# A diffusion transformer on one core: the first four chunks of the first stage one at a time

## The chip, the cores and the metric

The kernel runs on one core of a Trainium2 chip. The metric is the device time of one execution in microseconds. Engines are called by the names of the profile: PE is TensorE (matrix products), DVE VectorE, ACT ScalarE, POOL GpSimd, SP SyncE, whose queue issues most loads.

## What is computed

Two layers of a transformer on 256 latent tokens (x) and 256 context tokens (ctx) of 1024 features. Each layer first modulates its input with a scale and a shift per feature that come from a product of a conditioning vector with the adaLN weights (ada_w), then mixes tokens (retention in layer 0, neighbourhood attention in layer 1) and applies an MLP. The change is in the very first steps of layer 0:

```python
mod = (silu_c @ ada_w[i] + ada_b[i])[:, None, :]
mod_c = silu_cc @ ada_w[i] + ada_b[i]
sh1, sc1, g1, sh2, sc2, g2 = jnp.split(mod, 6, axis=-1)
...
h = x * (1.0 + sc1) + sh1
hc = ctx * (1.0 + sc1c) + sh1c
...
p = h @ w
q = heads(p[..., :qk_w], RET_QK_DIM)
...
v = heads(p[..., 2 * qk_w:2 * qk_w + v_w], RET_V_DIM)
```

All is in 32-bit floats. Each product with weights is done as three products of a rounded high part and a remainder (hi and lo of the weights, hTh and hTl of the tokens).

## The kernel before

The first stage computes, for head 0 of the retention, the query projection (256 columns, accumulated in the two banks pq) and the value projection (512 columns, accumulated for four groups of 128 tokens in the four banks pv). The 1024 features that both sum over are cut into eight chunks of 128. A chunk needs: its part of the shift and scale weights of adaLN (2 x 1024 x 128 floats, 1.05 MB), 128 columns of x and ctx (0.26 MB), and 128 rows of the projection weights (0.39 MB).

The work is done in quarters of two chunks (line 938). A quarter's adaLN weights come in four loads of 512 KB (tile rawq), its tokens in two loads (R), its projection weights in two (raw). For a quarter the engines do this:

- PE multiplies the adaLN weights by the conditioning columns cT in 32 short products that write into four strips of a bank (quarter_sums, line 802; tile pada). The profile counts each as two instructions, hence x64.
- DVE copies the sums out (quarter_row, tile row), PE adds the strips and turns the result into columns with two small products (quarter_columns, line 828, pada<-cst,row), and DVE adds the bias (tile mod).
- PE transposes the tokens of a chunk (chunk, tile pt).
- ACT and DVE modulate them (modulate_chunk, line 862): ACT writes both halves of hTh, DVE and ACT a half each of aff, DVE takes the difference to hTl. Each of these waits for the one before it.
- ACT rounds the projection weights (tile hi), DVE takes the remainder (lo).
- PE does the query products of a chunk (quarter_q, six of 512 columns) and its value products (quarter_v, three for each of the four token groups, a value block below).

The order on PE, ACT, DVE and SP in this stage is the order of the code. Value blocks of the chunk before are placed between the steps of the next quarter's modulation, so that PE has work while the chain from sums to modulated tokens runs through the other engines. The first quarter has nothing ahead of it: PE turns over products of a constant tile (turn_over, pq<-still) while it waits for loads. Loads are issued by SP in the order of need, a quarter or more ahead; a load waits where the tile that it fills is still in use. Raw projection weights have four buffers, adaLN quarters two slots (AQ), each of two tiles.

From line 996 on the same order of instructions holds on each engine with and without the change.

Of the kernel before, what the change touches and what calls it, by code (L numbers as in the profile page):

```python
# [10 lines left out]
F32 = mybir.dt.float32  # L11
# [6 lines left out]
P = 128  # L18
D = 1024
KC = D // P  # L20
# [73 lines left out]
def kernel(  # L94
# [50 lines left out]
    def bank(s="ps"):  # L145
        return psp.tile([P, 512], F32, tag="ps", name=nm(s))
# [104 lines left out]
            pending.append((lo[:], raw[:], hi[:]))  # L251
            units.append((hi, lo))

    def load():

        src, k, ncol = specs[loaded[0]]
        loaded[0] += 1
        raw = rawp.tile([P, k, ncol], F32, tag="raw", name=nm("raw"))
        sp.dma_start(out=raw[:], in_=src.rearrange("(k p) n -> p k n", p=P))

        def begin():
            hi = hip.tile([P, k, ncol], F32R, tag="hi", name=nm("hi"))
# [9 lines left out]
            return high, low  # L272

        return begin

    def lows(n=100, eng=None):
# [461 lines left out]
    pq = [bank("pq") for _ in range(2)]  # L738
    AQ = ((S_GS, S_SH), (S_SL, S_VH))

    def quarter_x(i, q):
        for a, src in enumerate((x, ctx_in)):
            cols = slice(256 * i, 256 * i + 256)
            q.dma_start(out=RR[a][:, :, cols], in_=src[0][:, cols].rearrange("(t p) c -> p t c", p=P))

    def quarter_loads(i):
        raws = ada_quarter_load(i, AQ[i % 2])
        quarter_x(i, sp)
        return raws

# [71 lines left out]
    def quarter_rows(i, raws):  # L822
        pr = bank("pada")
        for s in range(2):
            quarter_sums(pr, raws, s, range(KC))
        return pr, quarter_row(pr)
# [43 lines left out]
    def modulate_kinds(k, pts, between=lambda: None):  # L870

        tmp = scr("aff")
        for e, a in ((act, 0), (dve, 1)):
            modulated(e, hTh[:, k, KINDS[a]], pts[a][:, :NLAT], k, a)
        between()
        for e, a in ((act, 1), (dve, 0)):
            modulated(e, tmp[:, KINDS[a]], pts[a][:, :NLAT], k, a)
        dve.tensor_sub(out=hTl[:, k, :], in0=tmp[:], in1=hTh[:, k, :].bitcast(F32))

    def quarter_q(k, kk, wq, terms=range(3)):  # L880
        wh, wl = wq
        hh, hl = hs(k, 0, NT)
        for i in terms:
            w, h = ((wh, hh), (wl, hh), (wh, hl))[i]
            for dc in range(2):
                pe.matmul(
                    pq[dc][:], lhsT=w[:, kk, tsl(dc)], rhs=h, start=(k == 0 and i == 0), stop=(k == KC - 1 and i == 2)
                )
# [8 lines left out]
            for f in parts:  # L897
                f(k)

    raws = ada_quarter_load(0, AQ[0])  # L900
    quarter_x(0, sp)
    loads = [(load(), load())]
    raws1 = quarter_loads(1)
# [7 lines left out]
    quarter_sums(pr, raws, 0, range(0, KC))  # L911
    turn_over(1)
    quarter_sums(pr, raws, 1, range(0, 4))
    turn_over(1)
    quarter_sums(pr, raws, 1, range(4, KC))
    row = quarter_row(pr)
    turn_over(1)
    quarter_columns(pr, row, 0)
    pt0 = chunk_kinds(0)
    (qhigh, qlow), (vhigh, vlow) = (f() for f in loads[0])  # L920
    modulate_kinds(0, pt0, lambda: (qhigh(0), qlow(0)))
    wq, wv = take(2, 0)
    quarter_q(0, 0, wq, range(2))
    pt1 = chunk_kinds(1)
    quarter_q(0, 0, wq, (2,))
    vhigh(0)
    vlow(0)
    qhigh(1)
    modulate_kinds(1, pt1)
    qlow(1)  # L930
    vhigh(1)
    vlow(1)
    table_loads()
    raws = raws1
    pv = [bank("pv") for _ in range(4)]

    held_back = None
    for i in range(4):
        k = 2 * i
        if i < 2:  # L940
            raws2 = quarter_loads(i + 2)
            loads.append((load(), load()))
        if i:
            wq, wv = take(2, 0)
            quarter_q(k, 0, wq, range(2))
            quarter_v(k - 1, 1, held_back, range(3, 4))
            quarter_q(k, 0, wq, (2,))
        if i == 1:
# [4 lines left out]
        quarter_v(k, 0, wv)  # L953
        quarter_q(k + 1, 1, wq)
        if i == 3:
            ln_columns(rows)
            take(0, 3)
            quarter_v(k + 1, 1, wv)
            continue
        quarter_v(k + 1, 1, wv, range(1))  # L960
        held_back = wv
        (qhigh, qlow), (vhigh, vlow) = (f() for f in loads[i + 1])
        if i:
            qhigh(0)
            vhigh(0)
        pr, row = quarter_rows(i + 1, raws)
        if i:
            qlow(0)
            vlow(0)
        raws = raws2  # L970
        if i:
            pt = chunk(k + 2)
            quarter_columns(pr, row, k + 2)
            quarter_v(k + 1, 1, wv, range(1, 2))
        else:
            quarter_v(k + 1, 1, wv, range(1, 2))
            quarter_columns(pr, row, k + 2)
            pt = chunk(k + 2)
            qhigh(0)
            qlow(0)  # L980
        modulate_chunk(k + 2, pt)
        if not i:
            vhigh(0)
            vlow(0)
        quarter_v(k + 1, 1, wv, range(2, 3))
        modulate_chunk(k + 3, chunk(k + 3))
        qhigh(1)
        qlow(1)
        vhigh(1)
        vlow(1)  # L990
        if i == 1:
            make_strip(0, *tabs)
    act.on = dve.on = False

# [1218 lines left out]
```

## Time and profile before

| what | value |
|---|---|
| median of three runs | 1183.87 us (1182.28 to 1184.21) |
| the profiled execution, its own time | 1183.18 us |
| its span in the profile | 1181.4 us |
| PE busy | 1164.9 us, 99% |
| first product of the stage's projections | at 13.32 us |
| sums of quarters 1, 2, 3 start | at 20.48, 32.64, 44.55 us |
| end of the first stage's projections | 58.84 us |

A row of the timeline gives the start in us from the span's start, the length in us, the engine, the line (84 for all, since a helper issues them), the operation, the tiles (out<-in), the form and the number of instructions merged into it; in brackets stands how long the engine was idle just before, and what ended that. PEld is the loading of the stationary operand, which runs beside PE. A row of the windows gives the stretch, its length, the busy time and number of instructions of PE, PEld, DVE, ACT and POOL, the granted clock of PE, the busy share of the DMA engines and GB/s.

### The profile page before, as it was taken

Reading aid. Unit: us, or ns where it says so; the run is one execution under the profiler, and the core shown is the slowest. Engines: PE = TensorE matmul, PEld = TensorE weight load, DVE = VectorE, ACT = ScalarE, POOL = GpSimd, SP = SyncE. Lnnn points to the kernel's source line nnn. Section 1 sums busy time; section 2 is a strip of 40 time slices with the busy share of each in tenths; the row PEclk is TensorE's granted clock in tenths of the full one; section 3 lists DMA queues with packets and bytes.
Section 4 is the critical chain, followed back from the end, with each engine's and each line's share of the span. In section 5 each row is a group of like instructions: output and inputs, shape, how many; then the busy total and the mean of one; then the engine's idle time right before and its main releaser. Section 6 shows DMA issues by size and latency. Waiting matters only on the chain.

```text
span 1181.4 us, 17903 instructions
## 1 busy us (share of the span) xinstructions
PE 1164.9 (99%) x7042; PEld 983.3 (83%) x7042; DVE 809.8 (69%) x1292; ACT 482.8 (41%) x826; POOL 149.1 (13%) x174
## 2 busy tenths in 40 slices
PE   9999999999999999999999999999999999999996
PEld 6788888788888888888888888889788879999885
DVE  3575795698596376469888675568465588777546
ACT  3633432333323245332222433138366675555341
POOL 0102002100200240000202000230245200000002
PEclk9999999999999999999999999999999999999998
DMA  9742562865255213347775655646544443676861
GB/s 321 231 139 73 151 199 73 280 197 180 79 166 178 81 52 102 89 126 231 235 228 180 204 188 181 203 134 199 193 120 148 160 142 114 197 250 216 285 211 37
DMA packets 134469, 200.00 MB, mean 169 GB/s; under 512 B 16192, under 2 KB 76384, under 8 KB 134384
## 3 DMA queue, kind: packets, MB, share of 16 engines
q1 hardware_dynamic: 129552, 184.72, 49.3%
q0 software_dynamic: 3584, 11.59, 3.1%
q10 hardware_dynamic: 1248, 2.53, 0.6%
q8 instruction: 55, 0.90, 0.3%
q14 instruction: 30, 0.25, 0.1%
HBM read 190.31 MB, written 10.61 MB: 170 GB/s over the span
## 4 chain that ended last, share of the span: by engine, by line
PE 78%; DVE 2%; ACT 1%; POOL 0%; issue 0%; DVEq 0%; ACTq 0%
PE p L84 43%; PE pn L84 6%; PE pw L84 4%; PE pnv L84 4%; PE pv L84 4%; PE pg L84 4%; PE pq L84 4%; PE pnw L84 2%; PE ppt L84 2%; PE po L84 1%; PE pav L84 1%; PE pqk L84 1%; PE p1t L84 1%; PE pS L84 1%; PE pt L84 1%; DVE R L84 0%
## 5 line engine op out<-in xcount | busy, mean ns | idle before, releaser
L84 ACT CAST hi<-raw 128x1024 fp32r<-128x1024 f32 (+1 forms) x227 | 225.9, 1012 | 288.7 <-DMA raw<-in_mlp_w_dram 115.5
L84 DVE TENSOR_TENSOR lo<-raw,hi 128x1024 fp32r<-128x1024 f32 (+1 forms) x216 | 253.0, 1185 | 95.8 <-ACT hi L84 93.9
L84 PE MATMUL p<-hi,hid 128*128 128x512 f32 (+1 forms) x832 | 242.3, 374 | 0.0
L84 PEld LDWEIGHTS p<-hi,hid 128*128 128x128 f32 x832 | 152.2, 188 | 27.7
L84 PE MATMUL p<-hTh,hi 128*128 128x256 f32 (+1 forms) x512 | 170.0, 333 | 1.9 <-DVE r L84 1.9
L84 PE MATMUL p<-hTh,lo 128*128 128x256 f32 (+1 forms) x512 | 169.5, 332 | 0.3 <-DVE lo L84 0.3
L84 PE MATMUL p<-hTl,hi 128*128 128x256 f32 (+1 forms) x512 | 166.2, 329 | 0.0
L84 PE MATMUL p<-lo,hid 128*128 128x512 f32 (+1 forms) x416 | 155.3, 373 | 0.0
L84 DVE SCALAR_TENSOR_TENSOR acc<-rawa,scol,acc 128x1024 f32<-128x1024 f32 x63 | 81.2, 1308 | 44.9 <-DMA rawa<-in_ada_w_dram 44.8
L84 PEld LDWEIGHTS p<-hTh,hi 128*128 128x128 f32 x512 | 98.4, 192 | 10.8 <-DVE r L84 2.1
L84 PEld LDWEIGHTS p<-hTh,lo 128*128 128x128 f32 x512 | 98.4, 192 | 9.3 <-DVE lo L84 0.5
L84 PEld LDWEIGHTS p<-hTl,hi 128*128 128x128 f32 x512 | 96.2, 190 | 8.7
L84 PEld LDWEIGHTS p<-lo,hid 128*128 128x128 f32 x416 | 78.4, 188 | 13.6
L84 ACT CAST hid<-r 128x256 fp32r<-128x256 f32 (+1 forms) x64 | 32.0, 500 | 112.1 <-DVE r L84 111.9
L84 DVE SCALAR_TENSOR_TENSOR strips<-rawa,scol,strips 128x512 f32<-128x512 f32 x84 | 57.5, 744 | 0.0
L84 DVE TENSOR_TENSOR hid<-r,hid 128x256 fp32r<-128x256 f32 (+1 forms) x64 | 34.4, 538 | 26.7 <-ACT hid L84 26.7
L84 PE MATMUL pw<-hi,oh 128*128 128x512 f32 x128 | 51.0, 398 | 0.9 <-ACT oh L84 0.9
L84 PE MATMUL pg<-hi,hTh 128*128 128x512 f32 x128 | 50.7, 396 | 0.0
L84 PE MATMUL pv<-hi,hTh 128*128 128x512 f32 x128 | 50.4, 394 | 0.0
L84 PE MATMUL pw<-hi,ol 128*128 128x512 f32 x128 | 50.1, 391 | 0.0
L84 PE MATMUL pg<-hi,hTl 128*128 128x512 f32 x128 | 49.9, 390 | 0.0
L84 PE MATMUL pw<-lo,oh 128*128 128x512 f32 x128 | 49.9, 390 | 0.0
(234 smaller groups left out, 2169.0 us busy)
## 6 DMA issues: line engine op xcount, KB each, us to landing
raw<-in_mlp_w_dram SPq DMA_DIRECT2D x128, 512.0 KB
rawa<-in_ada_w_dram SPq DMA_DIRECT2D x80, 512.0 KB
raw<-in_ret_w_in_dram SPq DMA_DIRECT2D x46, 512.0 KB
raw<-in_nat_w_in_dram SPq DMA_DIRECT2D x24, 512.0 KB
rawq<-in_ada_w_dram SPq DMA_DIRECT2D x16, 512.0 KB
raw<-in_ret_w_o_dram SPq DMA_DIRECT2D x16, 512.0 KB
rpb_near<-far SPq DMA_DIRECT2D x20, 256.0 KB
bias<-rpb_near POOLq DMA_DIRECT2D x16, 320.0 KB, 3.8
```

The source lines that it names most:

```text
L84: r = f(*args, **kwargs)
```

## The change

The first four chunks (two quarters) are loaded, summed and modulated one at a time; quarters 2 and 3 stay quarters. For the first four chunks, the adaLN weights come in two loads of 512 KB a chunk, whose rows are 128 floats long instead of 256. The tokens of chunks 0 and 1 come in loads of 128 columns, and so do the projection weights of chunks 0 and 1, whose two tiles are filled in two parts each. The sums of a chunk are 16 short products, its columns one small product. Chunks 0 to 3 each have their own sums, row, columns and modulation. In the loop, which now runs over chunks, a value block stands between the sums and the transposes for quarters 2 and 3 as well, and the remainder of the value weights is taken after the modulation. Two of the ten turn_over products before the first query product go. The loads of the decay parameters, of the distance table and of the norm's rows, and the exponential's table, are placed after the modulation of chunks 1 and 2.

```diff
-    def load():
+    def load(whole=True):
...
-        sp.dma_start(out=raw[:], in_=src.rearrange("(k p) n -> p k n", p=P))
+        if whole:
+            sp.dma_start(out=raw[:], in_=src.rearrange("(k p) n -> p k n", p=P))
+
+        def part(i):
+            sp.dma_start(out=raw[:, i], in_=src[i * P : (i + 1) * P, :])
...
+    def ada_chunk_load(c):
+        raw = slot(AQ[c // 2][c % 2], [P, 2, KC, P], F32, "rawq")
+        for s in range(2):
+            w_ap = ada_w[0][:, s * D + P * c : s * D + P * c + P]
+            sp.dma_start(out=raw[:, s], in_=w_ap.rearrange("(k p) n -> p k n", p=P))
+        return raw
+
+    def chunk_sums(pr, raw, pairs):
+
+        for s, k in pairs:
+            j = 2 * (k % 2) + s
+            pe.matmul(
+                pr[32 * j : 32 * j + 32, :P], lhsT=cT[:, k, :, :].rearrange("p a t -> p (a t)"), rhs=raw[:, s, k, :],
+                start=(k < 2), stop=(k >= KC - 2), tile_position=(0, 32 * j),
+            )
+
+    def chunk_row(pr):
+        row = smp.tile([P, 256], F32, tag="row", name=nm("row"), bufs=1)
+        dve.tensor_copy(out=row[:, :P], in_=pr[:, :P])
+        return row
+
+    def chunk_columns(pr, row, c):
+        pe.matmul(pr[:, 256:260], lhsT=row[:, :P], rhs=cv("sel2"), start=True, stop=True)
...
+    ada = {0: ada_chunk_load(0)}
+    token_cols(0, P)
+    loads = [(load(False), load(False))]
+    for f in loads[0]:
+        f.part(0)
+    ada[1] = ada_chunk_load(1)
+    token_cols(P, P)
+    for f in loads[0]:
+        f.part(1)
+    ada[2] = ada_chunk_load(2)
+    token_cols(256, 256)
     loads.append((load(), load()))
+    ada[3] = ada_chunk_load(3)
...
+    for c in range(KC):
+        kk = c % 2
+        if c and c != 5:
+            if c % 2 == 0:
+                wq, wv = take(2, 0)
+            quarter_q(c, kk, wq, range(2))
+            quarter_v(*back, range(3, 4))
+            quarter_q(c, kk, wq, (2,))
+        if c in (1, 3):
+            ada[c + 3] = quarter_loads(c // 2 + 2)
             loads.append((load(), load()))
...
+        back = (c, kk, wv)
+        quarter_v(*back, range(1))
+        if c % 2:
+            parts = [f() for f in loads[c // 2 + 1]]
+        (qhigh, qlow), (vhigh, vlow) = parts
+        j = (c + 1) % 2
+        qhigh(j)
+        vhigh(j)
+        pr = bank("pada")
+        if c < 3:
+            chunk_sums(pr, ada[c + 1], [(s, k) for k in range(KC) for s in range(2)])
+            row = chunk_row(pr)
         else:
...
+        qlow(j)
+        quarter_v(*back, range(1, 2))
+        pt = chunk(c + 1)
+        (chunk_columns if c < 3 else quarter_columns)(pr, row, c + 1)
+        modulate_chunk(c + 1, pt)
+        vlow(j)
+        quarter_v(*back, range(2, 3))
+        if c > 2:
+            modulate_chunk(c + 2, chunk(c + 2))
+            for f in (qhigh, qlow, vhigh, vlow):
+                f(1)
```

How PE's order moves is seen at three places. In the rows, pq and pv are the query and value sums, pada the adaLN sums and columns, pt the transposes, and the number behind a name tells buffers apart.

PE before, from the last query products of chunk 1 (with the value products of chunk 0 all done) to the sums of quarter 1:

```order
L84 MATMUL pq_110<-hTl,hi_202 128x512
L84 MATMUL pq_111<-hTl,hi_202 128x512
L84 MATMUL pv_239<-hi_204,hTh 128x512
L84 MATMUL pv_239<-lo_205,hTh 128x512
L84 MATMUL pv_239<-hi_204,hTl 128x512
L84 MATMUL pada_280<-rawq_129,cT 32x128 x8
L84 MATMUL pada_280<-rawq_130,cT 32x128 x8
L84 MATMUL pada_280<-rawq_129,cT 32x128 x8
L84 MATMUL pada_280<-rawq_130,cT 32x128 x8
```

PE now, from the last product of chunk 0's first value block, through the sums, transposes and column of chunk 1, to its third value block:

```order
L84 MATMUL pv_199<-hi_189,hTl 128x512
L84 MATMUL pada_216<-rawq_126,cT 32x128 x16
L84 MATMUL pv_200<-hi_189,hTh 128x512
L84 MATMUL pv_200<-lo_190,hTh 128x512
L84 MATMUL pv_200<-hi_189,hTl 128x512
L84 MATMUL pt_239<-cst_81,R_100 128x128 x2
L84 MATMUL pt_239<-cst_81,R_101 128x128 x2
L84 MATMUL pada_216<-cst_81,row_233 128x4
L84 MATMUL pv_201<-hi_189,hTh 128x512
L84 MATMUL pv_201<-lo_190,hTh 128x512
L84 MATMUL pv_201<-hi_189,hTl 128x512
```

The sums that stood after the query products of two chunks now stand after the first value block of the first, and half as many of them.

PE before, from the column products of quarter 1 to the first query products of chunk 2:

```order
L84 MATMUL pada_280<-cst_81,row_313 128x4 x2
L84 MATMUL pt_321<-cst_81,R_100 128x128 x2
L84 MATMUL pt_321<-cst_81,R_101 128x128 x2
L84 MATMUL pv_241<-hi_204,hTh 128x512
L84 MATMUL pv_241<-lo_205,hTh 128x512
L84 MATMUL pv_241<-hi_204,hTl 128x512
L84 MATMUL pt_339<-cst_81,R_100 128x128 x2
L84 MATMUL pt_339<-cst_81,R_101 128x128 x2
L84 MATMUL pq_110<-hTh,hi_276 128x512
L84 MATMUL pq_111<-hTh,hi_276 128x512
```

PE now, from the transposes of chunk 2 to its first query products:

```order
L84 MATMUL pt_310<-cst_81,R_100 128x128 x2
L84 MATMUL pt_310<-cst_81,R_101 128x128 x2
L84 MATMUL pada_287<-cst_81,row_304 128x4
L84 MATMUL pv_201<-hi_189,hTh 128x512
L84 MATMUL pv_201<-lo_190,hTh 128x512
L84 MATMUL pv_201<-hi_189,hTl 128x512
L84 MATMUL pq_110<-hTh,hi_281 128x512
L84 MATMUL pq_111<-hTh,hi_281 128x512
```

The column product has moved behind the transposes, and the transposes of chunk 3, which stood between the value block and the query products, are gone from here.

PE before, at quarter 2, from its last sums to the second value block after them:

```order
L84 MATMUL pada_413<-rawq_244,cT 32x128 x8
L84 MATMUL pt_450<-cst_81,R_100 128x128 x2
L84 MATMUL pt_450<-cst_81,R_101 128x128 x2
L84 MATMUL pada_413<-cst_81,row_446 128x4 x2
L84 MATMUL pv_240<-hi_278,hTh 128x512
L84 MATMUL pv_240<-lo_279,hTh 128x512
L84 MATMUL pv_240<-hi_278,hTl 128x512
L84 MATMUL pv_241<-hi_278,hTh 128x512
```

PE now, at the same place:

```order
L84 MATMUL pada_422<-rawq_266,cT 32x128 x8
L84 MATMUL pv_200<-hi_283,hTh 128x512
L84 MATMUL pv_200<-lo_284,hTh 128x512
L84 MATMUL pv_200<-hi_283,hTl 128x512
L84 MATMUL pt_461<-cst_81,R_100 128x128 x2
L84 MATMUL pt_461<-cst_81,R_101 128x128 x2
L84 MATMUL pada_422<-cst_81,row_455 128x4 x2
L84 MATMUL pv_201<-hi_283,hTh 128x512
```

The value block that stood behind the column products stands ahead of the transposes.

More of the change, by code (lines that the diff above doesn't have):

```diff
@@ L272, in begin @@
             return high, low
+        begin.part = part
         return begin
@@ L739, with token_cols @@
     AQ = ((S_GS, S_SH), (S_SL, S_VH))
[L741 removed]
+    def token_cols(c0, n):
         for a, src in enumerate((x, ctx_in)):
[L743 to L744 removed]
+            cols = slice(c0, c0 + n)
+            sp.dma_start(out=RR[a][:, :, cols], in_=src[0][:, cols].rearrange("(t p) c -> p t c", p=P))
     def quarter_loads(i):
         raws = ada_quarter_load(i, AQ[i % 2])
[L748 removed]
+        token_cols(256 * i, 256)
         return raws
+    def ada_chunk_load(c):
[17 more added lines that the diff above has]
+        pe.matmul(pr[:, 256:260], lhsT=row[:, :P], rhs=cv("sel2"), start=True, stop=True)
+        dve.tensor_add(
+            out=mods[0, 0][:, :, c, :],
+            in0=pr[:, 256:260].rearrange("p (s t) -> p s t", s=2),
+            in1=bcol[:, :, c].unsqueeze(2).broadcast_to([P, 2, 2]),
+        )
     still = scr("still")
@@ L820, in quarter_row @@
         return row
[L822 to L826, printed above, removed]
     def quarter_columns(pr, row, c0):
@@ L910 @@
     turn_over(2)
-    quarter_sums(pr, raws, 0, range(0, KC))
+    chunk_sums(pr, ada[0], [(0, k) for k in range(KC)])
     turn_over(1)
[L913 to L918, printed above, removed]
+    chunk_sums(pr, ada[0], [(1, k) for k in range(KC)])
+    row = chunk_row(pr)
     pt0 = chunk_kinds(0)
-    (qhigh, qlow), (vhigh, vlow) = (f() for f in loads[0])
+    chunk_columns(pr, row, 0)
+    parts = [f() for f in loads[0]]
+    (qhigh, qlow), (vhigh, vlow) = parts
     modulate_kinds(0, pt0, lambda: (qhigh(0), qlow(0)))
     wq, wv = take(2, 0)
-    quarter_q(0, 0, wq, range(2))
-    pt1 = chunk_kinds(1)
-    quarter_q(0, 0, wq, (2,))
+    pv = [bank("pv") for _ in range(4)]
+    quarter_q(0, 0, wq)
     vhigh(0)
     vlow(0)
[L928 to L941, printed above, removed]
-            loads.append((load(), load()))
[L943 to L948, printed above, removed]
+    back = None
+    for c in range(KC):
[8 more added lines that the diff above has]
+            ada[c + 3] = quarter_loads(c // 2 + 2)
+            loads.append((load(), load()))
+        if c == 1:
+            table_loads()
+        if c == 2:
             act.dma_start(out=dt[:, 0], in_=dist)
@@ L952 @@
             sp.dma_start(out=cst1[:], in_=consts[:, NC0:])
[L953 to L958, printed above, removed]
-            continue
[L960 to L974, printed above, removed]
-        else:
[L976 to L991, printed above, removed]
+        if c in (4, 6):
+            quarter_v(c, kk, wv)
+            quarter_q(c + 1, 1, wq)
+            if c == 6:
+                ln_columns(rows)
+                take(0, 3)
+                quarter_v(c + 1, 1, wv)
+                break
+            continue
+        back = (c, kk, wv)
+        quarter_v(*back, range(1))
+        if c % 2:
+            parts = [f() for f in loads[c // 2 + 1]]
+        (qhigh, qlow), (vhigh, vlow) = parts
@@ new lines @@
+        j = (c + 1) % 2
[4 more added lines that the diff above has]
+            chunk_sums(pr, ada[c + 1], [(s, k) for k in range(KC) for s in range(2)])
+            row = chunk_row(pr)
+        else:
+            for s in range(2):
+                quarter_sums(pr, ada[c + 1], s, range(KC))
+            row = quarter_row(pr)
+        qlow(j)
+        quarter_v(*back, range(1, 2))
+        pt = chunk(c + 1)
+        (chunk_columns if c < 3 else quarter_columns)(pr, row, c + 1)
```

5 lines of the change are left out of this document (1 added, 4 removed).

## Prediction

> **What bounds the kernel now.** I read the page first, then the table of windows over the stretches of the first stage, then the timeline of TensorE, VectorE and ScalarE inside it.
>
> ```profile
> PE 1164.9 (99%) x7042; PEld 983.3 (83%) x7042; DVE 809.8 (69%) x1292; ACT 482.8 (41%) x826; POOL 149.1 (13%) x174
> ...
> 0.00:13.32 13.32, 11.01 (x93) 7.34 (x93) 2.21 (x10) 2.38 (x5) 0.19 (x4) 1.00 0.89 285
> 13.32:32.64 19.32, 19.23 (x143) 14.88 (x144) 9.62 (x19) 9.49 (x19) 0.70 (x3) 1.00 1.09 353
> 32.64:44.55 11.91, 11.91 (x113) 9.54 (x112) 6.14 (x13) 7.24 (x15) 4.32 (x4) 1.00 0.91 299
> 44.55:58.84 14.29, 14.29 (x123) 11.48 (x123) 7.59 (x14) 8.91 (x16) 0.00 (x0) 1.00 0.46 149
> 58.84:1181.40 1122.56, 1108.49 (x6573) 940.10 (x6571) 784.25 (x1238) 454.81 (x774) 143.87 (x163) 0.99 0.52 164
> ```
>
> TensorE is the bound of the whole span, and from 13.32 us, its first real product, to 58.84, where the stage ends, it is without work for only 0.09 us by these rows (their busy times include products whose modelled ends overlap, so short waits of a few tenths hide in it). After 58.84 the loads run at half their share. So a shift of the stage's end goes on to the end of the kernel nearly whole, and the stage can only get shorter in two ways: the first product comes earlier, or TensorE does less between it and the end. The first 13.32 us are the prize. Here is how that product comes about:
>
> ```profile
> 7.28 1.08 PE L84 MATMUL pada<-rawq,cT 128*32 128x128 f32 x32
> 8.29 0.70 PE L84 MATMUL pq<-still 128*128 128x256 f32 x2
> 8.91 0.38 PEld L84 LDWEIGHTS pada<-rawq,cT 128*32 128x32 f32 x16 [0.33 <-DMA rawq<-in_ada_w_dram]
> 9.49 0.70 PE L84 MATMUL pq<-still 128*128 128x256 f32 x2
> 10.30 0.38 PEld L84 LDWEIGHTS pada<-rawq,cT 128*32 128x32 f32 x16 [0.51 <-DMA rawq<-in_ada_w_dram]
> 11.01 0.42 DVE L84 COPY row<-pada 128x256 f32<-128x256 f32 x1 [3.96 <-PE pada L84]
> 11.49 0.61 PE L84 MATMUL pada<-cst,row 128*128 128x4 f32 x4
> 12.14 0.17 DVE L84 TENSOR_TENSOR mod<-pada,bcol 128x8 f32<-128x8 f32 x1 [0.70 <-PE pada L84]
> 12.41 0.56 ACT L84 ACTIVATE hTh<-pt,mod 128x256 fp32r<-128x256 f32 x1 [5.91 <-PE pt L84]
> 13.32 0.73 PE L84 MATMUL pq<-hTh,hi 128*128 128x512 f32 x2 [0.73 <-ACT hi L84]
> 15.62 0.39 PE L84 MATMUL pv<-hi,hTh 128*128 128x512 f32 x1
> ```
>
> The sums begin at 7.28 and wait twice for weights; the last 512 KB of them land at 10.30. From there a chain runs through four engines: sums, copy of the row, column products, addition, modulation, first product, 3.02 us after the landing. Every later group of features has the same chain, and what matters is what TensorE has to do meanwhile. The second quarter, and then the third:
>
> ```profile
> 20.48 1.95 PE L84 MATMUL pada<-rawq,cT 128*32 128x128 f32 x64
> 22.36 0.50 PE L84 MATMUL pv<-hi,hTh 128*128 128x512 f32 x1
> 22.60 0.41 ACT L84 CAST hi<-raw 128x256 fp32r<-128x256 f32 x1 [5.45 <-DMA raw<-in_ret_w_in_dram]
> 23.16 0.50 PE L84 MATMUL pada<-cst,row 128*128 128x4 f32 x4
> 23.53 0.63 PE L84 MATMUL pt<-cst,R 128*128 128x128 f32 x4
> 23.71 0.17 DVE L84 TENSOR_TENSOR mod<-pada,bcol 128x8 f32<-128x8 f32 x1 [0.78 <-PE pada L84]
> 23.92 0.48 PE L84 MATMUL pv<-hi,hTh 128*128 128x512 f32 x1
> 24.20 1.02 ACT L84 ACTIVATE hTh<-pt,mod 128x256 fp32r<-128x256 f32 x2 [1.20 <-PE pt L84]
> 25.27 0.73 PE L84 MATMUL pq<-hTh,hi 128*128 128x512 f32 x2
> 26.31 0.39 PE L84 MATMUL pv<-hi,hTh 128*128 128x512 f32 x1
> 27.18 0.74 PE L84 MATMUL pq<-hTl,hi 128*128 128x512 f32 x2
> 27.76 0.39 PE L84 MATMUL pv<-hi,hTh 128*128 128x512 f32 x1
> 28.22 0.39 PE L84 MATMUL pv<-hi,hTl 128*128 128x512 f32 x1
> 28.45 0.40 PE L84 MATMUL pv<-hi,hTh 128*128 128x512 f32 x1
> ...
> 32.64 1.95 PE L84 MATMUL pada<-rawq,cT 128*32 128x128 f32 x64
> 36.13 1.02 ACT L84 ACTIVATE hTh<-pt,mod 128x256 fp32r<-128x256 f32 x2 [1.40 <-DVE mod L84]
> 37.43 0.71 PE L84 MATMUL pq<-hTh,hi 128*128 128x512 f32 x2
> 39.14 0.69 PE L84 MATMUL pq<-hTl,hi 128*128 128x512 f32 x2
> ```
>
> In one quarter the chain is walked once for two chunks; one block of value products (three products, about 0.69 us) and a second set of transposes lie between the transposes at 23.53 and the product at 25.27.
>
> **The change part by part.**
>
> *Start: gain 2.4 us.* The first chunk needs 1.05 MB of modulation weights instead of 2.10. Two landings fix a line: 2.10 MB at 10.30, and the query weights of the second quarter, 6.29 MB in the queue's order, at 22.60, so 4.19 MB in 12.30 us, 0.341 MB/us. On it 1.05 MB lie there at 7.2, 1.31 MB (with tokens) at 8.0, 1.70 MB (with the chunk's projection weights) at 9.1. So the weights are there before their sums, which are not earlier than 7.28: what comes ahead of them (the columns of c) is unchanged. Eight sums are half of 8.29 - 7.28, 0.50 us, so 7.78; the warm-up product 8.91 - 8.29 - 0.33 = 0.30, so 8.1 for the second half; 0.71 (10.30 to 11.01) to the row copy, 8.8; the copy of half as many columns about 0.3, 9.1, and the transposes (0.4) fit beside it; one column product instead of two, about 0.5 instead of 0.65 to the addition, 9.7; 0.27 on to the modulation and 0.91 to the first product (12.14, 12.41, 13.32): 10.9. The rest of the first chunk goes as before, 2.30 us (13.32 to 15.62) to the value products, and the first block of them 0.80 with its end: the sums of chunk 1 start at 14.0. The two warm-up products that go were in idle time and are worth nothing.
>
> *Chunks 1, 2 and 3: a period of 7.24 us each.* Now each chunk walks the chain by itself. Counted from the start of its sums: 32 instead of 64 of the short sums, half of the 1.68 that 22.36 - 20.48 holds beyond 0.20 of issue, so 1.04; value block, 0.80 (22.36 to 23.16); transposes 0.39 (23.53 to 23.92); one column product, 0.25 at most. The addition comes about 0.45 after that product's start (two of them took 0.55, 23.16 to 23.71), at 2.68, and the modulation 0.20 later, at 2.88. From the modulation's start to the first product are 1.07 us (24.20 to 25.27), so that comes at 3.95; TensorE has by then one value block left, and it ends at 1.04 + 0.80 + 0.39 + 0.25 + 0.69 = 3.17. It waits 0.8. The last two query products come 2.98 after the modulation's start (24.20 to 27.18, the chain aff, aff, hTl), at 5.86, where the work between is done at 3.95 + 1.04 + 0.69 = 5.68: a wait of 0.2. Then 0.58 (27.18 to 27.76) and a value block with its change-over, 0.80: the next sums start at 7.24. The work in it is 6.3 us, the waits 0.96. Nothing covers them, since the second chunk's transposes, and the order columns first, transposes after, that covered them in a quarter are gone here.
>
> *The sum to the third quarter.* 14.0 + 3 x 7.24 = 35.7 us for the sums that start at 32.64 now: 3.1 us later. Of the 2.4 gained, 1.3 go into work that was ahead of the first product and now lies behind it (sums and column product of chunk 1), 2.5 into the waits, three times 0.96 against some 0.4 now (23.92 + 0.69 + 0.39 against 25.27, 26.31 + 0.69 against 27.18), 0.4 into the wait of chunk 0 that the transposes of chunk 1 filled, and the other 1.3 into change-overs between kinds of product, of which there are twice as many, about 0.1 each.
>
> *Quarters 2 and 3: 0.3 us each.* Their sums now are followed by a value block before transposes and columns. Modulation: 1.88 + 0.80 + 0.39 + 0.55 + 0.20 = 3.82 after the sums' start (3.49 now), last query products 2.98 later, 6.80, against 39.14 - 32.64 = 6.50. Twice 0.3.
>
> *Sum: 3.1 + 0.6 = 3.7 us slower.* The profiled execution took 1183.18 us (span 1181.4), which would become 1186.9; it lies 0.69 under the median 1183.87 of three, on which 3.7 gives 1187.6.
>
> *Loads.* By the line the weights of chunk 3's sums, 6.82 MB in, land at 24.1, while TensorE asks for them at 28.5; the third quarter's at 30.3 for 35.7. So the loads stay ahead and cost nothing, if short pieces move as fast. The first four chunks' rows are 512 bytes long instead of 1024, and no row of this trace has them alone. One end is the 353 GB/s at a share of 1.09 above, where nearly all pieces are 1 KB; the other is this stretch of 256-byte pieces:
>
> ```profile
> 505.00:511.00 6.00, 6.00 (x28) 4.99 (x27) 3.17 (x4) 2.35 (x4) 0.00 (x0) 1.00 0.35 57
> ```
>
> 57 / 0.35 x 1.09 = 178 GB/s at a full share. Taking the time of a piece as linear between 1.44 ns (256 bytes) and 2.90 (1024) gives 1.93 ns for 512, 265 GB/s. Then 4.72 MB of such pieces and 2.10 of others end at 28.1 (24.1 + 4.72 / 0.265 - 4.72 / 0.341), just before 28.5: cost 0 to 0.5. I take 0, since the nearer row is the one with pieces twice as long. The Trainium skill, "DMA: Bandwidth & Descriptors", Specifications, puts the shortest transfer at line rate at 512 bytes; by that the cost is nothing. Its section Bandwidth, on the other hand, asks for at least 1 MiB a transfer, which speaks against cutting tokens and weights into 128 KB; by its 2 us and bytes over 436 GB/s a 128 KB piece would take 2.3 us, 1.9 more than their share of the line, and the six of them one after another would add some 11 us. The trace disagrees where transfers queue behind each other: 353 GB/s with transfers of 256 and 512 KB.
>
> *What moves on ScalarE.* Loading of the exponential table and the issues of three small loads stand ahead of the casts of chunk 3, not behind them:
>
> ```profile
> 29.33 1.47 ACTq L84 DMA_DIRECT2D rows<-in_ln_b_dram  x1
> 29.85 1.28 ACT L84 ACT_TABLE_LOAD   x1
> ```
>
> Between the last modulation of chunk 2 and the first of chunk 3 are about 7.24 - 2.2 = 5.0 us; table, issues and casts (1.28 + 1.47 + 0.8 + 1.0) are 4.6. Covered, by 0.4; without cover at most 1.3. SP issues more, smaller loads in the same order; it runs ahead of the landings, so that costs nothing.
>
> **The rivals.** *The chain is hidden after all.* If the addition reaches ScalarE sooner or its two halves run closer, the 0.96 us of waits per chunk go and only the moved work stays: 3.7 - 2.9 = 0.8 slower, 1184.7 on the median, and within the measurement's reach. For it: now TensorE shows next to no waits at the same chain. Against: each step above is a duration from a row, and the block between is 0.69 against 1.27 to be covered. It decides if the waits are under 0.5 a chunk. *The lead lives:* all of the 2.4 us at the start are kept, because the smaller first loads let the whole stage run ahead, 1181.5. Against: the sums of chunk 1 alone take back 1.3, and TensorE has nothing else to drop. *The loads become the bound:* at 178 GB/s for short pieces chunk 3's weights land at 24.1 + 4.72 / 0.178 - 4.72 / 0.341 = 36.8, 8.3 us after they are asked for, and the sum is 12 us slower, 1195.9. For it only the 256-byte stretch, in which other limits may rule, as its share of 0.35 shows that the queue wasn't full.
>
> **How the numbers follow.** Forecast 0.61; chain hidden 0.27; lead kept 0.08; loads 0.04. The forecast's own terms are unsure by 0.15 us in each period's two waits and by 0.5 at the start and in the loads, so 2.4 to 6.5 us, 1186.3 to 1190.4; the range goes down to 1184.2 to take in most of the second case. A measurement of this kernel tells about 0.2%, 2.4 us, from no change. So slower by more: 0.64 (forecast, loads, less what ends under 2.4); within: 0.29; faster: 0.07.
>
> **What would show it.** Right: first query product near 10.9; sums of chunks 1, 2, 3 and of the third quarter at 14.0, 21.2, 28.5, 35.7; about 0.8 us of TensorE waiting for ScalarE's hTh and 0.2 for VectorE's hTl in each of the three periods; stage end near 62.5. Wrong: sums that wait for rawq, casts that hold up hTh (loads too late), periods near 6.3 (chain hidden), or an end of the stage that moves while the kernel's end does not.

## The result and the profile after

| what | before | after |
|---|---|---|
| median of nine runs each | 1183.16 us (1181.45 to 1184.21) | 1186.63 us (1185.06 to 1189.76) |
| ratio to before, 95% interval | | 1.0030 [1.0019, 1.0041] |
| the profiled execution, its own time | 1183.18 us | 1186.9 us |
| its span | 1181.4 us | 1185.1 us |
| first product of the projections | 13.32 us | 11.74 us |
| sums of quarters 2 and 3 start | 32.64, 44.55 us | 36.14, 48.43 us |
| end of the stage's projections | 58.84 us | 63.10 us |

The change costs 0.3%, some 3.5 us of the median; 3.7 was forecast. The table of windows of after, cut at the same events as that of before and with the period of chunk 1 as a stretch of its own at the end:

```profile
11.74:36.14 24.40, 22.29 (x177) 15.19 (x178) 10.02 (x22) 10.45 (x20) 3.35 (x5) 1.00 1.10 319
36.14:48.43 12.29, 12.20 (x114) 9.55 (x113) 6.13 (x13) 7.44 (x15) 1.70 (x2) 1.00 0.98 317
48.43:63.10 14.67, 14.57 (x123) 11.48 (x123) 7.40 (x14) 8.18 (x15) 0.00 (x0) 1.00 0.37 119
63.10:1185.10 1122.00, 1108.46 (x6573) 940.21 (x6571) 786.26 (x1238) 455.06 (x774) 147.20 (x163) 1.00 0.52 164
14.81:21.95 7.14, 6.62 (x57) 4.58 (x57) 2.62 (x6) 2.61 (x5) 0.00 (x0) 1.00 1.14 326
```

Between the first product and the stage's end TensorE was idle for 0.09 us before; now it is for 2.1 us up to the third quarter (24.40 - 22.29), and 0.5 in one period. After 63.10 it has the same 6573 instructions as before. The start, which answers to the block of before that began at 7.28, and the period of chunk 1 behind it:

```profile
7.12 1.07 PE L84 MATMUL pada<-rawq,cT 128*32 128x128 f32 x16
8.12 0.70 PE L84 MATMUL pq<-still 128*128 128x256 f32 x2
8.75 1.07 PE L84 MATMUL pada<-rawq,cT 128*32 128x128 f32 x16
9.75 0.66 PE L84 MATMUL pt<-cst,R 128*128 128x128 f32 x4
9.87 0.29 DVE L84 COPY row<-pada 128x128 f32<-128x128 f32 x1 [2.97 <-PE pada L84]
10.63 0.16 DVE L84 TENSOR_TENSOR mod<-pada,bcol 128x4 f32<-128x4 f32 x1 [0.48 <-PE pada L84]
11.74 0.73 PE L84 MATMUL pq<-hTh,hi 128*128 128x512 f32 x2 [1.15 <-ACT hi L84]
14.04 0.40 PE L84 MATMUL pv<-hi,hTh 128*128 128x512 f32 x1
14.81 1.08 PE L84 MATMUL pada<-rawq,cT 128*32 128x128 f32 x32
15.82 0.50 PE L84 MATMUL pv<-hi,hTh 128*128 128x512 f32 x1
...
17.20 0.49 PE L84 MATMUL pv<-hi,hTh 128*128 128x512 f32 x1
17.38 0.16 DVE L84 TENSOR_TENSOR mod<-pada,bcol 128x4 f32<-128x4 f32 x1 [0.80 <-PE pada L84]
17.58 1.02 ACT L84 ACTIVATE hTh<-pt,mod 128x256 fp32r<-128x256 f32 x2 [1.99 <-DVE mod L84]
18.65 0.73 PE L84 MATMUL pq<-hTh,hi 128*128 128x512 f32 x2 [0.49 <-ACT hTh L84]
20.55 0.73 PE L84 MATMUL pq<-hTl,hi 128*128 128x512 f32 x2
```

No sum waits for rawq any more. But the two halves of chunk 0's sums take as long each (7.12 to 8.12, 8.75 to 9.75) as all sums of chunk 1 (14.81 to 15.82). In chunk 1 the chain of single steps is open to view: copy, column product, addition at 17.38, modulation at 17.58, product at 18.65, while the one value block begun at 17.20 keeps TensorE busy for 0.69 us, to 17.89. It stands for 0.76 us; the row's 0.49 is less because the modelled ends of products reach into the wait. The list of TensorE's waits from 5 to 64 us (total, times, longest) has this three times, once for each of chunks 1 to 3, and no load but one at the very start (the wait for hi lies ahead of the first query product, that for hTl inside chunk 0):

```profile
PE pq L84 <- ACT hTh L84: 1.5, 3, 0.5
PE pq L84 <- ACT hi L84: 1.1, 1, 1.1
PE pc L84 <- DMA crow<-in_ada_b_dram: 0.6, 1, 0.6
PE pq L84 <- DVE hTl L84: 0.5, 1, 0.5
```

### The profile page after: what moved, and what is told of

Its sections match the earlier page's. It is cut to its first block, busy times and chain, and to the rows that moved or that the text cites. A ratio compares the mean times of both kernels' runs of the same rounds, so it can differ in the third digit from the quotient of the medians.

```text
span 1185.1 us, 17898 instructions
## 1 busy us (share of the span) xinstructions
PE 1166.0 (98%) x7038; PEld 982.7 (83%) x7038; DVE 811.9 (69%) x1295; ACT 483.5 (41%) x827; POOL 152.4 (13%) x174
## 4 chain that ended last, share of the span: by engine, by line
PE 78%; DVE 2%; ACT 1%; POOL 0%; issue 0%; DVEq 0%; ACTq 0%
PE p L84 43%; PE pn L84 6%; PE pw L84 4%; PE pnv L84 4%; PE pv L84 4%; PE pg L84 4%; PE pq L84 4%; PE pnw L84 2%; PE ppt L84 2%; PE po L84 1%; PE pav L84 1%; PE pqk L84 1%; PE p1t L84 1%; PE pS L84 1%; PE pt L84 1%; DVE R L84 0%
## 5 line engine op out<-in xcount | busy, mean ns | idle before, releaser
L84 PE MATMUL pq<-hTh,hi 128*128 128x512 f32 x128 | 49.2, 394 | 2.8 <-ACT hTh L84 1.5
L84 POOL DMA_DIRECT2D grow<-grow x6 | 3.4, 565 | 368.6 <-DVE grow L84 368.6
```

What stands on the lines that cost most here:

```text
L84: r = f(*args, **kwargs)
```

## The experiments

The theory from the two traces: three terms make the loss, which are chunk 0's sums on two strips at a time, the chain that nothing covers in chunks 1 to 3, and the value block ahead of the transposes in quarters 2 and 3. The rival: the loads with short rows set the pace, and what is taken away on TensorE comes back as a wait for weights. For each run the table gives the median, the number of runs, the ratio to before with its interval, and of the profiled execution the first product and the end of the stage.

| kernel | median us (runs) | ratio to before | first product | stage end |
|---|---|---|---|---|
| the change | 1186.63 (9) | 1.0030 [1.0019, 1.0041] | 11.74 | 63.10 |
| e1_strips | 1185.2 (10) | 1.0031 [1.0021, 1.0040] | 10.69 | 62.37 |
| e2_quarters | 1185.54 (10) | 1.0024 [1.0014, 1.0034] | 11.54 | 61.99 |
| e3_chunks | 1185.48 (7) | 1.0024 [1.0013, 1.0035] | 12.47 | 63.35 |
| e4_narrow | 1185.46 (10) | 1.0027 [1.0017, 1.0038] | 16.86 | 65.05 |
| e5_all | 1182.99 (11) | 1.0007 [0.9998, 1.0016] | 10.91 | 60.81 |
| e6_narrow_warm | 1185.93 (11) | 1.0028 [1.0019, 1.0037] | 16.05 | 62.53 |
| e7_warm | 1185.68 (7) | 1.0032 [1.0021, 1.0042] | 11.77 | 63.14 |
| e8_all_warm | 1182.81 (11) | 1.0002 [0.9993, 1.0011] | 10.62 | 60.26 |

The kernel before had a median of 1182.54 (28 runs) beside e1 to e4 and of 1182.78 (29 runs) beside e5 to e8. By the medians the experiments lie closer together than by the ends of the stage; the last section but one shows why.

**e1_strips: the sums of chunk 0 on four strips in turn.** The order of all other sums, taken for the first chunk too:

```diff
-    turn_over(2)
-    chunk_sums(pr, ada[0], [(0, k) for k in range(KC)])
-    turn_over(1)
-    chunk_sums(pr, ada[0], [(1, k) for k in range(KC)])
+    turn_over(3)
+    chunk_sums(pr, ada[0], [(s, k) for k in range(KC) for s in range(2)])
```

> The changed kernel, with the 16 sums of chunk 0 issued as those of chunks 1 to 3 are, over four strips in turn instead of two strips at a time; the warm-up product between the halves goes ahead of them. Theory (two strips take as long for 8 sums as four strips for 16: 1.00 us from 7.12 to 8.12 for 8): the sums take 1.0 us instead of 2.0, the first query product comes at 10.7 instead of 11.74, and the stage ends 0.5 to 1.0 us earlier than 63.10, less than 1.0 if the weights of chunk 1's sums are not there by 13.8. Rival (the second half of chunk 0's weights sets the pace, not the strips): the sums wait for a load, and the first query product stays within 0.3 us of 11.74. Time: 0.5 to 1.0 us under the changed kernel.

Timeline of e1_strips from its first sums to its first product, and at chunk 2:

```profile
7.36 1.41 PE L84 MATMUL pada<-rawq,cT 128*32 128x128 f32 x32
7.69 0.81 PEld L84 LDWEIGHTS pada<-rawq,cT 128*32 128x32 f32 x30 [0.20 <-DMA rawq<-in_ada_w_dram]
8.69 0.66 PE L84 MATMUL pt<-cst,R 128*128 128x128 f32 x4
10.69 0.50 PE L84 MATMUL pq<-hTh,hi 128*128 128x512 f32 x1 [1.14 <-ACT hi L84]
```

```profile
20.89 1.08 PE L84 MATMUL pada<-rawq,cT 128*32 128x128 f32 x32
21.98 0.41 ACT L84 CAST hi<-raw 128x256 fp32r<-128x256 f32 x1 [3.24 <-DMA raw<-in_ret_w_in_dram]
23.42 0.62 ACT L84 CAST hi<-raw 128x512 fp32r<-128x512 f32 x1 [1.03 <-DMA raw<-in_ret_w_in_dram]
23.47 0.16 DVE L84 TENSOR_TENSOR mod<-pada,bcol 128x4 f32<-128x4 f32 x1 [0.62 <-PE pada L84]
23.95 1.01 ACT L84 ACTIVATE hTh<-pt,mod 128x256 fp32r<-128x256 f32 x2
25.02 0.50 PE L84 MATMUL pq<-hTh,hi 128*128 128x512 f32 x1 [0.79 <-ACT hTh L84]
```

From the first sum to the transposes are 1.33 us (7.36 to 8.69) instead of 2.63 (7.12 to 9.75), and the first product comes 3.33 us after the first sum instead of 4.62. The sums of chunk 1 start 1.05 earlier, at 13.76. So the first term is what the theory says. The 1.33 us hold a short wait: the sums now need both loads of chunk 0 from the start, go on at 7.69 when the second is there, and take 1.00 from then on (7.69 to 8.69). Part of the gain is given back at once: in chunk 2 ScalarE's cast waits for its weights until 21.98 and that of the value weights until 23.42, and the modulation behind them starts 0.48 us after the addition's start (23.47 to 23.95) instead of 0.20; TensorE waits 0.79, and this period is 7.37 us instead of 7.11. The stage ends 0.73 earlier. These waits for loads are the rival's first signs.

**e2_quarters: the old order of transposes and columns for quarters 2 and 3.**

```diff
-        quarter_v(*back, range(1, 2))
+        early = c > 2
+        if not early:
+            quarter_v(*back, range(1, 2))
         pt = chunk(c + 1)
         (chunk_columns if c < 3 else quarter_columns)(pr, row, c + 1)
+        if early:
+            quarter_v(*back, range(1, 2))
```

> The changed kernel, with the transposes and column products of quarters 2 and 3 ahead of the value block again, as before the change. Theory (that order costs 0.38 us in each of the two quarters, through later modulation): the distances from sums to sums and from the last sums to the stage's end go from 12.29 and 14.67 back to 11.91 and 14.29, the stage ends at 62.3 instead of 63.10, 0.8 us less time. Rival (quarters are longer because their weights come later): both distances stay at 12.29 and 14.67 and a load is what TensorE or the casts wait for.

Timeline of e2_quarters at quarter 2, then the modulation of after at the same place, where the sums start at 36.14:

```profile
35.94 1.95 PE L84 MATMUL pada<-rawq,cT 128*32 128x128 f32 x64
...
39.29 1.02 ACT L84 ACTIVATE hTh<-pt,mod 128x256 fp32r<-128x256 f32 x2 [1.59 <-DVE mod L84]
...
47.77 1.96 PE L84 MATMUL pada<-rawq,cT 128*32 128x128 f32 x64
```

```profile
40.01 1.02 ACT L84 ACTIVATE hTh<-pt,mod 128x256 fp32r<-128x256 f32 x2 [2.50 <-DVE mod L84]
```

The modulation comes 3.35 us after the sums' start instead of 3.87, and the quarter takes 11.83 instead of 12.29; quarter 3 takes 14.22 (47.77 to 61.99) instead of 14.67. So the third term is shown, 0.45 a quarter, even a little more than the 0.38 by which these quarters had grown over before.

**e3_chunks: the same for the three chunks.** Transposes and column product come first, and the value block behind them joins the one that is already there, so that two value blocks, 1.38 us, lie between the column and the first query product.

```diff
-        quarter_v(*back, range(1, 2))
+        early = c < 3
+        if not early:
+            quarter_v(*back, range(1, 2))
         pt = chunk(c + 1)
         (chunk_columns if c < 3 else quarter_columns)(pr, row, c + 1)
+        if early:
+            quarter_v(*back, range(1, 2))
```

> The changed kernel, with the transposes and column product of chunks 1, 2 and 3 ahead of the value block, so that two value blocks instead of one cover the way from the columns to the modulated tokens. Theory (the exposed chain is what the chunks cost): the wait of 0.9 us ahead of each chunk's first query product goes to under 0.2, the period from sums to sums falls from 7.1 to about 6.35 us, and the stage ends 1.5 to 2.3 us earlier than 63.10, at 60.8 to 61.6; less than 2.3 where the casts of chunk 2 or the weights of chunk 3 come too late for the earlier order. Rival (loads set the periods): the wait moves to the sums or to the casts, and the stage's end moves by less than 0.5.

Timeline of e3_chunks, chunk 2 from its sums to those of chunk 3:

```profile
23.51 1.08 PE L84 MATMUL pada<-rawq,cT 128*32 128x128 f32 x32
25.62 1.02 ACT L84 ACTIVATE hTh<-pt,mod 128x256 fp32r<-128x256 f32 x2 [1.44 <-DVE mod L84]
26.70 0.73 PE L84 MATMUL pq<-hTh,hi 128*128 128x512 f32 x2
29.95 0.32 PE L84 MATMUL pada<-rawq,cT 128*32 128x128 f32 x4
```

The modulation starts 2.11 us after the sums instead of 2.77, the wait for hTh is gone from the row at 26.70, and chunk 2's period is 6.44 us (23.51 to 29.95) instead of 7.11. The next is 6.46. The second term is shown in the periods: 0.65 us a chunk of the 0.76. The stage, however, ends at 63.35 and not at 60.8 to 61.6 as expected. This execution's sums started late, at 7.85, and between 14 and 18 us TensorE's granted clock was low (chunk 1's period, 6.90, lies partly in it):

```profile
14.00:18.00 4.00, 3.83 (x37) 2.69 (x37) 0.72 (x2) 1.02 (x2) 0.00 (x0) 0.57 1.19 300
```

The times don't show the whole gain either: the three runs of e3 with a mean granted clock of 0.997 have a median of 1185.0 us, 0.8 under the 1185.81 of the change's five, where three periods would give 2.0. How much of the term reaches the end of the kernel is therefore not shown by this run; e5 has it again.

**e4_narrow and e6_narrow_warm: the kernel before with the change's short rows alone.** The loads of the first two quarters are cut into 128 columns; sums, modulation and order on all engines stay as in before. A part of the edit:

```diff
+    def narrow_load(i, ss):
+        raws = [slot(ss[h], [P, 2, KC, P], F32, "rawq") for h in range(2)]
+        for s in range(2):
+            for h, raw in enumerate(raws):
+                c0 = s * D + 256 * i + P * h
+                w_ap = ada_w[0][:, c0 : c0 + P]
+                sp.dma_start(out=raw[:, s], in_=w_ap.rearrange("(k p) n -> p k n", p=P))
+        return raws
...
-        raws = ada_quarter_load(i, AQ[i % 2])
+        raws = (narrow_load if i < 2 else ada_quarter_load)(i, AQ[i % 2])
```

> The kernel before, with the narrow loads alone: adaLN weights and tokens of the first two quarters in rows of 128 floats, everything else as before. Theory (pieces of 512 bytes move at about 265 GB/s, and the changed kernel only hides that by asking for less at first): the first query product comes at 14.5 to 15.2 instead of 13.32, the sums of the second quarter wait for their weights and come at 23.5 to 24.5 instead of 20.48, the stage ends 3 to 4.5 us later than 58.84, and the time is 3 to 4.5 us over the kernel before. Rival (short pieces cost nothing): all within 0.5 us of the kernel before.

e6 is e4 with more turn_over products in the waits of the start, to keep the clock up:

```diff
-    turn_over(1)
+    turn_over(8)
     quarter_sums(pr, raws, 1, range(0, 4))
...
     pt0 = chunk_kinds(0)
+    turn_over(2)
```

> The kernel before with the narrow loads alone, as in the run with that edit, and warm-up products put into the waits that they make (eight instead of one behind the first half of the sums, two behind the transposes). Theory (there two things came together: loads about 2 us later, and TensorE's granted clock at half from 13 to 22 us after a stretch with little work): the granted clock stays at 1.00, the first query product comes at 15.2 to 15.9 instead of 16.86, the sums of the second quarter at 22.4 to 23.5 instead of 26.40, the stage ends at 61 to 62 instead of 65.05, and no run is more than 5 us over the kernel before. Rival (the loads alone make it 6 us): the stage ends near 65 with the clock at 1.00.

Windows of e4_narrow, and then of e6_narrow_warm:

```profile
14.00:18.00 4.00, 3.27 (x13) 2.62 (x12) 1.89 (x5) 2.11 (x5) 0.00 (x0) 0.50 1.21 294
18.00:22.00 4.00, 4.00 (x13) 3.22 (x12) 2.93 (x7) 1.76 (x4) 0.00 (x0) 0.50 1.22 292
```

```profile
14.00:18.00 4.00, 3.92 (x23) 2.86 (x22) 2.74 (x7) 2.67 (x6) 0.00 (x0) 1.00 1.20 296
18.00:22.00 4.00, 4.00 (x19) 3.28 (x19) 2.84 (x6) 1.14 (x3) 0.00 (x0) 1.00 1.17 281
```

At a full share (1.20 to 1.22) the short rows move 292 to 296 GB/s, where the rows of before, mostly of 1 KB, moved 353 at 1.09. In before's order that is dear, since the first quarter needs all of its weights: at a full clock (e6) the first product comes at 16.05 instead of 13.32 and the stage ends 3.7 us later, at 62.53. Some 0.6 of this is not the rows' but that of the eight added products, which hold the sums until 11.80, where in e4 the load let them go on at 11.21; and 1.0 is lost in quarter 2 (12.91 us against 11.91), whose casts wait for weights. Both runs are later than expected: in e4 a first product at 14.5 to 15.2 and a stage end 3 to 4.5 us behind before's (it is 6.2), in e6 15.2 to 15.9 and 61 to 62. In the changed kernel the same loads are there in time for TensorE, since the first chunk asks for half as much. The two kernels also differ in the clock, 0.50 against 1.00 from 14 to 22 us, and the stage ends 2.5 us earlier in e6. The medians (1185.46, 1185.93) don't show that, since only three of e4's ten runs, the profiled one among them, have a mean clock of 0.991 or 0.992, and the others 0.996 or 0.997.

**e5_all: the three edits together,** and the cast of the value weights behind the modulation for the chunks:

```diff
-        vhigh(j)
+        if c > 2:
+            vhigh(j)
...
-        quarter_v(*back, range(1, 2))
         pt = chunk(c + 1)
         (chunk_columns if c < 3 else quarter_columns)(pr, row, c + 1)
+        quarter_v(*back, range(1, 2))
         modulate_chunk(c + 1, pt)
+        if c < 3:
+            vhigh(j)
```

> The changed kernel with the three repairs together: chunk 0's sums over four strips in turn, transposes and columns ahead of the value block for all chunks and quarters, and the cast of a chunk's value weights behind its modulation. Theory (the chain between the engines, the strips and the quarters' order are all that the change lost): sums of chunk 1 near 13.8 us, three periods of 6.45, sums of the third quarter near 33.1, two of 11.9, the stage ends near 59.3 against 63.10 with the change and 58.84 without it; time 0 to 1 us over the kernel before. Rival (once the chain is covered the loads take over, since short rows move slower): the periods of chunks 2 and 3 stay near 7 us with waits for a load, the stage ends at 60.3 or later.

Timeline of e5_all at quarter 2:

```profile
33.94 1.96 PE L84 MATMUL pada<-rawq,cT 128*32 128x128 f32 x64
36.24 0.40 ACT L84 CAST hi<-raw 128x256 fp32r<-128x256 f32 x1 [4.21 <-DMA raw<-in_ret_w_in_dram]
37.08 0.17 DVE L84 TENSOR_TENSOR mod<-pada,bcol 128x8 f32<-128x8 f32 x1
37.65 0.62 ACT L84 CAST hi<-raw 128x512 fp32r<-128x512 f32 x1 [1.00 <-DMA raw<-in_ret_w_in_dram]
38.18 1.01 ACT L84 ACTIVATE hTh<-pt,mod 128x256 fp32r<-128x256 f32 x2
```

With the chain covered, periods of 6.43, 6.80 and 6.72 us bring the third quarter's sums to 33.94, and now the loads are late. ScalarE idles 4.21 us ahead of its cast at 36.24, up to the landing of the weights, and another microsecond ahead of the next; the addition is done at 37.25, but the modulation stands behind that second cast until 38.18. This quarter takes 12.66 us (to 46.60) instead of e2's 11.83. The stage ends at 60.81, not at the 59.3 that the three terms alone would give. Of these 1.5 us, 0.83 lie in this quarter and 0.37 in chunk 2, whose cast waits in the same way; the other 0.3 are chunk 3's, where the load is in time but DVE's hTl takes 0.97 us instead of 0.69, beside work of GpSimd on the tile dt. Whether that work is the cause was not tried; in the changed kernel hTl (at 34.05) took 0.69 beside the same GpSimd instruction. (The Trainium skill, "SBUF — State Buffer", Terms, says that these two engines share a pair of ports, and that the one which loses it is blocked for the other's whole instruction. The GpSimd instruction took 1.51 us and hTl only 0.28 more than elsewhere, so the trace doesn't show that, and no run here tests it.) Theory and rival are each partly right: the terms are real, and as soon as they are gone, 1.2 us come back where casts wait for loads. The kernel is back at the time of before, 1.0007 [0.9998, 1.0016].

**e7_warm and e8_all_warm: products of a constant tile in the wait ahead of the first product,** in the changed kernel (e7) and in e5 (e8, with two of them ahead of its sums instead of three).

```diff
     chunk_columns(pr, row, 0)
+    turn_over(3)
     parts = [f() for f in loads[0]]
```

> The changed kernel with three warm-up products more, in the 1.15 us that TensorE waits ahead of its first query product. Theory (a part of the changed kernel's runs loses some us to the halved clock, which the emptier start makes likelier): the profiled places stay within 0.3 us of the changed kernel's, counted from the start of the sums, and the slow runs over 1188 us become rarer, median 0 to 0.7 us lower. Rival (the clock plays no part in the changed kernel's time): the same spread of runs and the same median within 0.3 us.

> The three repairs together, with one warm-up product less ahead of the sums and three in the wait ahead of the first query product. Theory: as the repairs alone, 0.3 us earlier from the sums on, stage end near 59.0, time within 1 us of the kernel before, to either side; a gain over it is not expected, since sums, columns and change-overs are more work than in quarters. Rival (loads): as for the repairs alone, no earlier than 60.3.

e7 leaves the stage as it was (first product 11.77, end 63.14); whether it moves the time is not settled, since three of its seven runs lie at 1187.2 to 1188.0 (mean clock 0.996) and four at 1185.3 to 1185.7 (0.997). e8 ends the stage at 60.26, where 59.0 was expected, and has the median of before, 1.0002 [0.9993, 1.0011]. No version beats the kernel before.

## Why the prediction was right

*Start: gain 2.4.* This is the step that failed, by its size: the gain is 1.6. "Eight sums are half of 8.29 - 7.28, 0.50 us" took the time of short products from a group that writes four strips in turn. Chunk 0's halves write two strips each, and eight sums take 1.00 us, twice. The warm-up between them took 0.63 (8.12 to 8.75) where 0.30 was taken: the prediction subtracted the 0.33 of idle time at 8.91 as a wait for a load, but the same 0.33 stands ahead of the second half now, with no load to wait for. The steps behind it hold: the copy 0.29 for 0.3, copy to product 1.87 for 2.1, product to value products 2.30 as forecast. e1 shows the strips to be the cause by removing them.

*Chunks 1, 2 and 3: 7.24 each.* Measured 7.14, 7.11 and 7.08. By steps for chunk 1, counted from its sums: addition 2.57 (forecast 2.68), modulation 2.77 (2.88), first product 3.84 (3.95), a wait of 0.76 (0.8), last query products 5.74 (5.86), and a wait of 0.18 ahead of them (0.2; 20.55 less the end of the work before it, 20.14 + 0.23). The step that decided against the rival "hidden after all" is thus right, each number within 0.12 us, and e3 shows that the order transposes, column, value block would have hidden it. The "lead lives" failed for the reason given: chunk 1's sums and the waits took the gain back by the third quarter, which starts 3.5 us later than before.

*Quarters: 0.3 each.* Measured 0.38 each (12.29 against 11.91, 14.67 against 14.29), shown by e2.

*The sum.* Stage end 4.26 later against 3.7: 0.8 from the start, 0.4 less in the periods, 0.16 more in the quarters. That the median then moved by 3.5, nearer to 3.7 than the stage's end, is luck: the next section shows that the part behind the stage changes its length by itself by more than this.

*Loads: cost 0.* Right for the changed kernel, whose casts in the loop wait but never the products, and by a small margin. The line of 0.341 MB/us, from longer rows, was too fast for these: it had both loads of chunk 0 there at 7.2, and in e1 the sums wait for the second until 7.69. For 512-byte rows the estimate of 265 GB/s was nearer than line rate:

```profile
9.00:10.00 1.00, 1.00 (x18) 0.80 (x14) 0.13 (x1) 0.00 (x0) 0.00 (x0) 1.00 1.21 292
```

This window of after, in which only short rows are loaded, shows 292 GB/s at a share of 1.21, some 17% under the 353 of before at a share of 1.09. The rule of the Trainium skill weighed in the prediction ("DMA: Bandwidth & Descriptors", Specifications: line rate from 512 bytes on) is not borne out here.

## What the runs showed of the hardware

**The granted clock falls to half after waits far under 3 us, and where a wait lies decides.** Near 453 us every one of these kernels has one wait of TensorE for DVE's r, 1.9 us long. In each of the ten traces the changes of the granted clock lie whole multiples of 3.413 us apart; in before the clock is up from 6.00, down from 453.14, up from 456.56 and down from 1173.35 to the end, which makes 131, 1 and 210 of them. Windows of before laid on this grid, and then of e8_all_warm, where the same wait ends at 454.29:

```profile
449.73:453.14 3.41, 1.51 (x13) 1.30 (x12) 3.06 (x5) 1.91 (x5) 0.00 (x0) 1.00 0.33 112
453.14:456.56 3.42, 3.42 (x18) 3.42 (x17) 2.28 (x6) 1.80 (x7) 0.00 (x0) 0.50 0.52 163
```

```profile
452.92:456.33 3.41, 2.04 (x17) 2.05 (x18) 2.47 (x6) 1.38 (x4) 0.00 (x0) 1.00 0.33 87
456.33:459.74 3.41, 3.41 (x31) 3.41 (x30) 1.55 (x5) 1.10 (x3) 0.00 (x0) 1.00 0.25 81
```

In before the whole wait lies in one stretch of the grid, TensorE is busy for 1.51 us of it, and the next stretch runs at 0.50: its products start 0.21 us apart. In e8 a border cuts the wait, 2.04 us of work are left in the second of the two stretches, and the products start 0.12 apart from the second on. The ten traces agree on this: up to the last products each of the eight stretches with 1.92 us of work or less is followed by half clock, and none with 1.99 or more is; the stretch ahead of the last fall has 0.88 us or less. Six of the eight hold the wait near 453 us; the others are e3's from 10.76 to 14.17 (1.76), into which two waits of 1.14 and 0.51 fell, and e4's from 9.16 to 12.58 (1.92). The clock is back after one stretch, in e4 after three.

Of the ten profiled executions six show the low stretch near 453 us (before, after, e3, e4, e5, e6) and four don't (e1, e2, e7, e8). What lies behind the stage, span less stage end, is 1120.5 to 1120.7 us in the four and 1121.4 to 1122.6 in the six. The four are those whose mean granted clock over the whole execution is 0.997, the six have 0.991 to 0.996, and among runs of one kernel the mean clock goes with the time: before at 0.997 or more has a median of 1181.5 (10 of 28 runs) and 1181.4 (9 of 29), at 0.995 and 0.996 about 1183. Compared at 0.997 or more alone, the times follow the end of the stage: the change 4.3 us over before (5 of 9 runs) for a stage end 4.3 later, e1 3.2 for 3.5, e2 3.2 for 3.2, e5 1.6 for 2.0, e6 3.1 for 3.7, e7 4.0 for 4.3, e8 1.3 (10 of 11 runs) for 1.4 (the profiled executions of e3 and e4 had low stretches in the stage itself, so their stage ends can't be set beside these times). So at one clock the change costs somewhat more than its median says, and e8 equals before only because it has the low stretch so seldom. Why the wait falls well for e8 in ten of eleven runs is open: the grid begins at another place in each trace (the clock first goes up between 4.33 and 7.34 us), and only one run of each kernel has a trace.

The Trainium skill, "TensorE: Matmul & The Clock Gate", Part 1, states that half clock follows an idle window of about 3.4 us whose start runs freely, so that the moment varies. The length of the window and its free start agree with the traces. That it has to be idle doesn't: 1.50 to 1.92 us of work in it did not keep the clock up.

**Short products that share strips are slower.** Eight products of 128 x 128 on two strips in turn took 1.00 us (7.12 to 8.12 in after), eight on four strips 0.57 (8.92 to 9.49 in before) and sixteen on four strips 1.01 (14.81 to 15.82).

## What to carry to other kernels

A chain through several engines has a fixed length, here 1.07 us from the modulation to the product and as much again ahead of it (9.75 to 10.83 in chunk 0); cutting a batch in halves walks it twice as often, so count for each half what independent work lies inside the chain, and put that work behind the chain's last step on the bound engine, not ahead of it. A smaller first piece brings the first product forward only by what the bound engine does not have to do later instead: here TensorE was 1.6 us ahead at 12 us and 3.5 behind at 36. And before taking a short duration from a row, see that the group it comes from has the same pattern of destinations.
